# The last output part of a decoder layer's first feed-forward: loads asked for together, the third weight set summed and split ahead of two updates, and copies of the turned x on two engines

## The chip, the cores and the metric

The kernel runs on one core of one Trainium2 chip. The metric is device time in microseconds (us), as the median of several executions. TensorE (PE in the profile, PEld for its weight loads) multiplies into PSUM; VectorE (DVE) and ScalarE (ACT) do the elementwise work; GpSimd (POOL) and SyncE (SP) start most of the DMAs. Every engine takes its own instructions in the order in which they were written into its queue.

## The reference

One decoder layer over 512 tokens of width 1024, in float32: a gated feed-forward, a mixer (a state-space head group and a differential attention), a cross-attention into a memory of 256 tokens, a second gated feed-forward and a last norm.

```python
x = x + 0.5 * swiglu(rms_norm(x, norm_ffn1_w[l]), ffn1_w_in[l], ffn1_w_out[l])
x = x + hybrid_mixer(rms_norm(x, norm_mix_w[l]), ...)
x = x + memory_cross_attention(rms_norm(x, norm_cross_w[l]), rms_norm(mem, norm_mem_w[l]), ...)
x = x + 0.5 * swiglu(rms_norm(x, norm_ffn2_w[l]), ffn2_w_in[l], ffn2_w_out[l])
...
def swiglu(h, w_in, w_out):
    gate, up = jnp.split(h @ w_in, 2, axis=-1)
    return (jax.nn.silu(gate) * up) @ w_out
```

The change is in the product with `ffn1_w_out` and in what follows it directly.

## The kernel before

Every float32 operand is split into a high part (`wh`, `s31h`, ..., a copy on ScalarE) and a low part (`wl`, `s31l`, ..., source minus high, on VectorE), and each product is three passes on TensorE: high by high, low by high, high by low. The products of both feed-forwards are block products of 2 by 2 blocks with seven products in place of eight (the Strassen-Winograd form), so sums of blocks are needed on both sides: `S1` to `S4`.

The first feed-forward goes in three thirds of its 2816 hidden columns. A third first makes quads (`quad`, L260, tiles `qa`, `qe`, `qb`), which give the gated hidden blocks `th`. From the last `th` of a third the steps in `block_tiles` and `sums_in_steps` (L205) make `g11`, `s31`, `s24` and `g` with their high and low parts. Then `out_blocks` (L1287) multiplies them with the output weights into six PSUM tiles, `oa`, `oe` and `ob` for two halves each. In the last third there are four blocks k = 0 to 3, in two parts (0, 1) and (2, 3); only k = 3 comes from the last `th`. The order of the seven products is:

- `oa` with block 11 and `oe` with `S1`, part after part: 11 first part, `S1` first part, 11 second part, `S1` second part;
- a copy of `oa` into `ob` on ScalarE (L1392), two updates of `x` from `oe` on VectorE (`update`, L1334), then `ob` with `S2` ("the third weight set");
- a copy of `ob` to `u` on ScalarE (L1399) and a subtraction from `oe` on VectorE, then `oa` with block 12, `ob` with `S3`, `oe` with `S4`, `ob` with block 22, each with updates of `x` behind it.

One set of a part is 128 x 1024, loaded to a tile `wr` (512 KB) and split to `wh` and `wl`; there are six `wr` and three of each of the others. In the first feed-forward the sums of weights are made in the kernel: `S1`'s set is a load of B12 by SyncE and an adding DMA of B11 by GpSimd on top (`added`, L1342); the third set is `S1`'s plus B22, by one VectorE instruction per part (`t2`, L1353, L1355); `S3`'s is a load and an adding DMA; the set for block 22 adds B21 to the third set, in the last third by DMA (`t4`, L1366). Each matmul of these products is 128 x 512 (L1319).

Between them stand other streams: `prepare` puts four small matmuls `prel` and two ScalarE copies `hot` (L640) with two DMAs (L643) into the last third; `memory_in` (L1069) puts eight splits of the memory, `hm`, there. Behind the third, `turn` (L1251) turns x by 32 TensorE transposes into eight PSUM tiles `pxf` and copies them back (L1258); the norm of x follows (`nboth`, `nv`, `ncol`, `ndiag`, then two matmuls `nrow`), and the keys of the memory (`pck`, L146). SyncE's and GpSimd's queues stand in the order of the source; on the other engines the framework sets the order from its own model of times, and a wait is put in wherever data or a buffer asks for it. The last third of the first feed-forward is the only one with `by_dma`. The second feed-forward uses the same `out_blocks` with weight sums that lie in DRAM.

Of the kernel before, what the change touches and what calls it, by code (L numbers as in the profile page):

```python
# [18 lines left out]
T = 512  # L19
# [81 lines left out]
def body(tc, a, dbg=None):  # L101
# [38 lines left out]
    last, start, last_sum, recent, newest, newest_mm, first_block = [], [], [], [], [], [], []  # L140
# [64 lines left out]
    def sums_in_steps(b11, b21, b22, b12, pair=None):  # L205
# [9 lines left out]
        s31 = split("s31", s31)  # L215
        yield
# [852 lines left out]
    def memory_in(dst):  # L1069
        yield 9.0  # L1070
# [180 lines left out]
    def turn(n, banks=None, summed=False):  # L1251
# [5 lines left out]
        for tb in range(4):  # L1257
            S.activation(x[4 * n + tb], pt[tb], AF.Copy)  # L1258
            if summed:
                squared(4 * n + tb, x[4 * n + tb])  # L1260
            yield
# [25 lines left out]
    def out_blocks(blocks, sums, g, col4, ncol4, each=None, finale=None, clean=True, n=None, by_dma=False):  # L1287
# [14 lines left out]
        def weights(of, part, raw=None):  # L1302
# [5 lines left out]
            recent[:] = [i.ins for i in split_into(hi, lo, raw)]  # L1308
# [13 lines left out]
        def product(ps, of, which, first=False, ready=None, after=((), ())):  # L1322
            for part in parts:
                if ready and part == parts[0]:
                    w = ready
# [27 lines left out]
        def t2(part):  # L1353
            more = fetch(blocks[B22], part)
            V.tensor_tensor(t_raw[part], t_raw[part], more, ALU.add)  # L1355
            return t_raw[part]
# [11 lines left out]
        later = {}  # L1368
        here = sums is None
        if here:  # L1370
            sums = [t1, added(blocks[B12], blocks[B22], "gate"), t2, lambda part: t_raw[part]]
        ready = [None, None]
        if early:
            ready = [weights(of, parts[0]) for of in (blocks[B11], sums[0])]
            yield
        bank = [acc, aux]
# [5 lines left out]
        both = [product(a_ps, blocks[B11], "11", True, ready[0]), product(e_ps, sums[0], S1, True, ready[1], ((), tuple(first_block)))]  # L1382
# [18 lines left out]
        yield from product(a_ps, b21 if here and not by_dma else blocks[B21], "12")  # L1401
# [5 lines left out]
        for n, _ in enumerate(product(b_ps, sums[1], S3, after=(copies, ()))):  # L1407
            if n == 0:
                first_split = list(recent)
            elif n == 12 and by_dma:  # L1410
                with behind(first_split):
                    for part in t_raw:
                        t4(part)
            yield
# [182 lines left out]
```

## Time and profile before

| what | us |
|---|---|
| median of 3 runs (lowest, highest) | 1299.35 (1299.22, 1300.01) |
| the profiled execution | 1299.78 |
| its span | 1298.0 |
| TensorE busy in it | 1284.4 |
| VectorE, ScalarE, GpSimd busy | 970.5, 710.2, 119.1 |

A profile's times count from the start of the span. A row of a timeline has the start, the busy time, the engine, the line, the operation, the tile written and the tiles read, the count of instructions merged in the row, and in brackets the idle time of the engine ahead of it with what ended it. Rows overlap a little, since an instruction's end is its result's, while the engine takes the next one sooner. A row of the waits has the total, the times and the longest. A row of the windows has the stretch, its length, the busy time of an engine with its instructions, the clock that was granted to TensorE (1.00 is full), the share of the DMA engines and GB/s.

### The profile page before, as it was taken

Reading aid. Unit: us, or ns where it says so; the run is one execution under the profiler, and the core shown is the slowest. Engines: PE = TensorE matmul, PEld = TensorE weight load, DVE = VectorE, ACT = ScalarE, POOL = GpSimd, SP = SyncE. Lnnn points to the kernel's source line nnn. Section 1 sums busy time; section 2 is a strip of 40 time slices with the busy share of each in tenths; the row PEclk is TensorE's granted clock in tenths of the full one; section 3 lists DMA queues with packets and bytes.
Section 4 is the critical chain, followed back from the end, with each engine's and each line's share of the span. In section 5 each row is a group of like instructions: output and inputs, shape, how many; then the busy total and the mean of one; then the engine's idle time right before and its main releaser. Section 6 shows DMA issues by size and latency. Waiting matters only on the chain.

```text
span 1298.0 us, 20081 instructions
## 1 busy us (share of the span) xinstructions
PE 1284.4 (99%) x7709; PEld 1125.5 (87%) x7709; DVE 970.5 (75%) x1543; ACT 710.2 (55%) x1207; POOL 119.1 (9%) x149
## 2 busy tenths in 40 slices
PE   9999999999999999999999999999999999999997
PEld 7889998998888778877888888889899899989995
DVE  6988897797776676567867696645678878877886
ACT  7544564565654564346644574434466546555554
POOL 1001010001101011100102011020001000000000
PEclk9999999999999999999999999999999999999999
DMA  9468777777975436653475567693249876666662
GB/s 336 101 172 209 183 195 207 227 192 203 295 234 155 131 65 159 227 165 98 106 207 180 158 163 223 198 228 113 66 130 249 214 223 183 185 191 191 173 206 94
DMA packets 69264, 234.75 MB, mean 181 GB/s; under 512 B 8161, under 2 KB 9665, under 8 KB 68817
## 3 DMA queue, kind: packets, MB, share of 16 engines
q1 hardware_dynamic: 53200, 180.91, 41.8%
q0 software_dynamic: 13168, 45.67, 19.8%
q10 hardware_dynamic: 2800, 6.91, 1.6%
q8 instruction: 60, 0.98, 0.3%
q14 instruction: 36, 0.29, 0.1%
HBM read 231.30 MB, written 48.29 MB: 215 GB/s over the span
## 4 chain that ended last, share of the span: by engine, by line
PE 81%; issue 12%; DMA 2%; DVE 2%; POOL 1%; ACT 1%; POOLq 0%; SPq 0%; ACTq 0%; DVEq 0%
PE qb L242 11%; PE pm L146 10%; PE qe L242 8%; PE qa L242 8%; PE pxbc L146 5%; PE ob L1319 5%; PE oa L1319 4%; PE pcq L146 3%; PE oe L1319 3%; PE pz L146 3%; PE pk L146 2%; PE pq L146 2%; PE pa L146 2%; PE pcv L146 2%; PE pv L146 2%
## 5 line engine op out<-in xcount | busy, mean ns | idle before, releaser
L155 ACT ACTIVATE wh<-wr 128x1024 fp32r<-128x1024 f32 (+1 forms) x323 | 328.2, 1018 | 304.6 <-PE qe L242 37.2
L156 DVE TENSOR_TENSOR wl<-wr,wh 128x1024 fp32r<-128x1024 f32 (+1 forms) x323 | 378.4, 1175 | 99.7 <-ACT wh L155 73.0
L788 ACT ACTIVATE ec<-ec,mn 128x512 f32<-128x512 f32 (+3 forms) x64 | 35.4, 554 | 22.0 <-DVE mn L787 22.0
L787 DVE CUSTOM_DVE_ANT_0 ec<-ps,bias 128x512 f32<-128x512 f32 (+3 forms) x64 | 28.1, 487 | 16.1 <-PE ps L146 15.9
L900 DVE SCALAR_TENSOR_TENSOR conv<-pxbc,par,conv 128x511 f32<-128x511 f32 (+2 forms) x48 | 35.7, 744 | 3.5 <-ACT conv L896 2.9
L251 POOL DMA_DIRECT2D wr<-in_f2q x11 | 9.7, 879 | 307.7 <-DMA wr<-in_f2q 116.8
L366 POOL TENSOR_TENSOR ncol<-nv,mhalf 128x4 f32<-128x4 f32 (+1 forms) x9 | 11.0, 1222 | 291.1 <-DVE nv L364 291.1
L146 PE MATMUL pxbc<-hnl,wh 128*128 128x512 f32 x128 | 35.6, 404 | 0.0
L146 PE MATMUL pxbc<-hnh,wh 128*128 128x512 f32 x128 | 35.3, 400 | 0.0
L146 PE MATMUL pxbc<-hnh,wl 128*128 128x512 f32 x128 | 32.3, 393 | 0.0
L453 DVE TENSOR_TENSOR gate<-qb,row 128x512 f32<-128x512 f32 x19 | 13.1, 692 | 22.1 <-PE qb L242 22.1
L146 PEld LDWEIGHTS pxbc<-hnh,wl 128*128 128x128 f32 x128 | 23.8, 188 | 5.3 <-issue 0.2
L251 POOL DMA_DIRECT2D wr<-in_f1q x16 | 14.0, 873 | 152.2 <-DMA wr<-in_f1q 58.9
L146 PEld LDWEIGHTS pxbc<-hnl,wh 128*128 128x128 f32 x128 | 23.2, 188 | 4.7 <-issue 0.4
L146 PEld LDWEIGHTS pxbc<-hnh,wh 128*128 128x128 f32 x128 | 23.0, 189 | 4.6 <-issue 0.5
L454 ACT ACTIVATE gate<-gate 128x1024 f32<-128x1024 f32 x19 | 20.1, 1057 | 10.9 <-DVE gate L453 10.9
L146 PE MATMUL pv<-wh,hnh 128*128 128x512 f32 x64 | 25.3, 395 | 0.0
L146 PE MATMUL pv<-wh,hnl 128*128 128x512 f32 x64 | 25.2, 393 | 0.0
L855 POOL TENSOR_TENSOR rr<-ev,mhalf 128x4 f32<-128x4 f32 x8 | 8.3, 1034 | 163.1 <-DVE ev L853 163.1
L155 ACT ACTIVATE s31h<-s 128x512 fp32r<-128x512 f32 x30 | 18.7, 624 | 7.4 <-DVE s L212 4.4
L155 ACT ACTIVATE s24h<-s 128x512 fp32r<-128x512 f32 x30 | 18.8, 625 | 7.0 <-DVE s L214 7.0
L301 ACT ACTIVATE u<-qb 128x512 f32<-128x512 f32 x19 | 11.4, 598 | 19.8 <-PE qb L242 19.8
(461 smaller groups left out, 3527.9 us busy)
## 6 DMA issues: line engine op xcount, KB each, us to landing
wr<-in_f2q SPq DMA_DIRECT2D x44, 512.0 KB, 4.4
wr<-in_f1q SPq DMA_DIRECT2D x40, 512.0 KB, 4.3
wr<-in_f1b SPq DMA_DIRECT2D x25, 512.0 KB, 5.3
isum<-in_f2q SPq DMA_DIRECT2D x22, 512.0 KB, 5.4
wr<-isum SPq DMA_DIRECT2D x22, 512.0 KB, 4.2
wsum<-in_f2b SPq DMA_DIRECT2D x20, 512.0 KB, 6.3
wr<-wsum SPq DMA_DIRECT2D x20, 512.0 KB, 4.4
wr<-in_f1q POOLq DMA_DIRECT2D x16, 512.0 KB, 6.5
```

The source lines that it names most:

```text
L146: newest_mm[:] = [nc.tensor.matmul(out, w, x, start=start, stop=stop).ins]
L155: S.activation(hi, src, AF.Copy),
L156: V.tensor_tensor(lo, src, hi.bitcast(F32), ALU.subtract),
L242: newest_mm[:] = [nc.tensor.matmul(out, w_[:, wc], xs[kp][which][x_], start=first and j == 0 and f == 0 and kp == 0, stop=j == 2 and kp == ...
L251: last_sum[:] = [G.dma_start(raw, m, accum_op=ALU.add).ins]
L301: copy = S.activation(u2, b_ps, AF.Copy)
L453: V.tensor_tensor(gate[:, 2 * i : 2 * i + 2], halves(gs[i]), row, ALU.mult)
L454: S.activation(gate, gate, AF.Silu)
L787: V.tensor_tensor_reduce(out=ec[:, :n], in0=ps[c][:, parts[i]], in1=bias[:, T - n :], scale=0.125, scalar=3e38, op0=ALU.add, op1=ALU.min, ...
L788: S.activation(ec[:, :n], ec[:, :n], AF.Exp, bias=mn, scale=-1.0, accum_out=sm[c][:, i : i + 1])
L900: V.scalar_tensor_tensor(y[:, d:], ps[:, : T - d], par[:, cw + j : cw + j + 1], y[:, d:], ALU.mult, ALU.add)
L1319: newest_mm[:] = [nc.tensor.matmul(ps, a_[:, ts], b_[:, ws], start=first and k == 0 and j == 0, stop=k == n - 1 and j == 2, skip_group_che ...
```

## The change

Four edits, the first two in `out_blocks`:

1. `ask_early`, for the last third alone: the second parts of block 11 and `S1` are asked for, then B22 for both parts in four loads of 256 KB to tiles of their own (`more`), then both parts of `S3`'s set with their adding DMAs. Before, each load stood in the queue where its product was written. The additions of B22 (`t2`) become four instructions of 128 x 512 in place of two of 128 x 1024. The adding DMAs of `t4` are asked for in the product with block 12, no longer in the one with `S3`.
2. The third weight set is made (`weights`) ahead of the copies of `oa` and the two updates of x: both parts in the last third, the first part everywhere else. The low half of its first part is told to stand behind the low half of `s31` (`sums_low`); in the last third the two updates stand behind the split.
3. `turn` with banks: four of its eight copies go to VectorE.
4. `memory_in` starts 13 units of the model's time after its cue in place of 9.

```diff
+        sums_low[:] = last[1:]
...
     def memory_in(dst):
-        yield 9.0
+        yield 13.0
...
         for tb in range(4):
-            S.activation(x[4 * n + tb], pt[tb], AF.Copy)
+            if banks and tb % 2:
+                V.tensor_copy(x[4 * n + tb], pt[tb])
+            else:
+                S.activation(x[4 * n + tb], pt[tb], AF.Copy)
...
-        def weights(of, part, raw=None):
+        def weights(of, part, raw=None, low_behind=()):
...
-            recent[:] = [i.ins for i in split_into(hi, lo, raw)]
+            high = S.activation(hi, raw, AF.Copy)
+            with behind(low_behind):
+                low = V.tensor_tensor(lo, raw, hi.bitcast(F32), ALU.subtract)
+            recent[:] = [high.ins, low.ins]
...
         def t2(part):
-            more = fetch(blocks[B22], part)
-            V.tensor_tensor(t_raw[part], t_raw[part], more, ALU.add)
+            more = pieces.pop(part) if part in pieces else (fetch(blocks[B22], part),)
+            n = t_raw[part].shape[1] // len(more)
+            for i, m in enumerate(more):
+                V.tensor_tensor(t_raw[part][:, i * n : (i + 1) * n], t_raw[part][:, i * n : (i + 1) * n], m, ALU.add)
             return t_raw[part]
...
+        def ask_early():
+            for of, make in ((B11, lambda part: fetch(blocks[B11], part)), (S1, t1)):
+                asked[of, parts[1]] = make(parts[1])
+            for part in parts:
+                pieces[part] = [s2("more") for _ in range(*part)]
+                for k, m in zip(range(*part), pieces[part]):
+                    nc.sync.dma_start(m, blocks[B22][:, k * T : (k + 1) * T])
+            for part in parts:
+                asked[S3, part] = seventh(part)
...
+        if by_dma:
+            ask_early()
...
+        third = {part: weights(sums[2], part, low_behind=() if n else sums_low) for n, part in enumerate(parts if by_dma else parts[:1])}
+        third_split = list(recent) if by_dma else []
         for t in range(2):
             S.activation(b_ps[t], a_ps[t], AF.Copy)
-        for t in range(2):
-            update(t + 2, 1, e_ps[t], 1, False)
-        yield from product(b_ps, sums[2], S2)
+        with behind(third_split):
+            for t in range(2):
+                update(t + 2, 1, e_ps[t], 1, False)
+        yield from product(b_ps, sums[2], S2, ready=third)
...
-        yield from product(a_ps, b21 if here and not by_dma else blocks[B21], "12")
+        for n, _ in enumerate(product(a_ps, b21 if here and not by_dma else blocks[B21], "12")):
+            if n == 12 and by_dma:
+                for part in t_raw:
+                    t4(part)
+            yield
```

What this makes of the queues, at the places that the prediction speaks of. First VectorE, in the last third, from the low half of `S1`'s second set (the first `wl`) to the updates of x. Before, with `wr_3373` and `wr_3459` the sets of the first and second part, to which L1355 adds B22:

```order
L156 TENSOR_TENSOR wl_3463<-wr_3459,wh_3462 128x1024
L213 TENSOR_TENSOR s_598_3392<-s_597_3391,th_3381 128x256
L1355 TENSOR_TENSOR wr_3373<-wr_3373,wr_3492 128x1024
L214 TENSOR_TENSOR s_598_3392<-s_598_3392,th_3381 128x256
L156 TENSOR_TENSOR s31l_3397<-s_597_3391,s31h_3396 128x512
L1355 TENSOR_TENSOR wr_3459<-wr_3459,wr_3516 128x1024
L156 TENSOR_TENSOR s24l_3401<-s_598_3392,s24h_3400 128x512
L156 TENSOR_TENSOR wl_3496<-wr_3373,wh_3495 128x1024
L156 TENSOR_TENSOR gl_3405<-th_3381,gh_3404 128x512
L1336 SCALAR_TENSOR_TENSOR x_123<-oe_3410,col_68_292,x_123 128x512
```

And VectorE there now, with `wr_3373` and `wr_3410` as the two sets and `more` as B22:

```order
L1314 TENSOR_TENSOR wl_3477<-wr_3410,wh_3476 128x1024
L213 TENSOR_TENSOR s_598_3392<-s_597_3391,th_3381 128x256
L214 TENSOR_TENSOR s_598_3392<-s_598_3392,th_3381 128x256
L156 TENSOR_TENSOR s31l_3397<-s_597_3391,s31h_3396 128x512
L156 TENSOR_TENSOR s24l_3401<-s_598_3392,s24h_3400 128x512
L156 TENSOR_TENSOR gl_3405<-th_3381,gh_3404 128x512
L1364 TENSOR_TENSOR wr_3373<-wr_3373,more_3413 128x512
L1364 TENSOR_TENSOR wr_3373<-wr_3373,more_3414 128x512
L1364 TENSOR_TENSOR wr_3410<-wr_3410,more_3417 128x512
L1364 TENSOR_TENSOR wr_3410<-wr_3410,more_3418 128x512
L1314 TENSOR_TENSOR wl_3502<-wr_3373,wh_3501 128x1024
L1314 TENSOR_TENSOR wl_3508<-wr_3410,wh_3507 128x1024
```

All additions now stand behind `s31l`, `s24l` and `gl`, where one stood ahead of `s31l` and the other ahead of `s24l`; both low halves of the third set follow them, ahead of the updates.

ScalarE at the same place, before, from the high half of `S1`'s second set to the second part of the third set (`wh_3495` and `wh_3519` are the third set's high halves):

```order
L155 ACTIVATE wh_3462<-wr_3459 128x1024
L155 ACTIVATE s31h_3396<-s_597_3391 128x512
L155 ACTIVATE wh_3495<-wr_3373 128x1024
L155 ACTIVATE s24h_3400<-s_598_3392 128x512
L1392 ACTIVATE ob_3412<-oa_3408 128x512
L1392 ACTIVATE ob_3413<-oa_3409 128x512
L155 ACTIVATE gh_3404<-th_3381 128x512
L640 ACTIVATE hot_2459<-prel_3473 8x256
L640 ACTIVATE hot_2460<-prel_3473 8x256
L643 DMA rel_d<-hot_2459 8x256
L159 ACTIVATE hm_3478<-mem_539_3032,par 128x256
L159 ACTIVATE hm_3504<-mem_539_3032,par 128x256
```

And ScalarE there now (`wh_3501` and `wh_3507` are the third set's high halves):

```order
L1312 ACTIVATE wh_3476<-wr_3410 128x1024
L155 ACTIVATE s31h_3396<-s_597_3391 128x512
L155 ACTIVATE s24h_3400<-s_598_3392 128x512
L155 ACTIVATE gh_3404<-th_3381 128x512
L1420 ACTIVATE ob_3431<-oa_3427 128x512
L1420 ACTIVATE ob_3432<-oa_3428 128x512
L641 ACTIVATE hot_2459<-prel_3487 8x256
L641 ACTIVATE hot_2460<-prel_3487 8x256
L644 DMA rel_d<-hot_2459 8x256
L644 DMA rel_d<-hot_2460 8x256
L1312 ACTIVATE wh_3501<-wr_3373 128x1024
L1312 ACTIVATE wh_3507<-wr_3410 128x1024
```

The high half of the third set's first part has moved from the third place of this piece behind the two `hot` copies, which read `prel`, and behind both DMAs.

VectorE in the first third of the second feed-forward, before (`wl_10673` is the third set's first part, `wl_10691` its second):

```order
L156 TENSOR_TENSOR wl_10673<-wr_10670,wh_10672 128x1024
L156 TENSOR_TENSOR s31l_10583<-s_2167_10577,s31h_10582 128x512
L156 TENSOR_TENSOR wl_10691<-wr_10688,wh_10690 128x512
L156 TENSOR_TENSOR s24l_10587<-s_2168_10578,s24h_10586 128x512
L1336 SCALAR_TENSOR_TENSOR x_123<-oe_10600,col_2175_10594,x_123 128x512
```

And now (`wl_10675` is the third set's first part):

```order
L156 TENSOR_TENSOR s31l_10589<-s_2169_10583,s31h_10588 128x512
L1314 TENSOR_TENSOR wl_10675<-wr_10672,wh_10674 128x1024
L156 TENSOR_TENSOR s24l_10593<-s_2170_10584,s24h_10592 128x512
L1343 SCALAR_TENSOR_TENSOR x_123<-oe_10606,col_2177_10600,x_123 128x512
L156 TENSOR_TENSOR gl_10597<-th_10573,gh_10596 128x512
```

Here `s31l` and the third set's low half have changed places; the second part's has gone behind both updates.

Elsewhere: TensorE's queue is the same but for the two matmuls `nrow` of the memory's norm, which stood directly behind the 32 transposes and now stand behind the first 18 `pck`, and those of x's norm, which stand two `pck` earlier, counted in `pck`. In SyncE's queue the four `more` loads stand behind the first four loads of `out_blocks`, whose order is as before; behind them `S3`'s two loads, then the two of B21. The eight `hm` splits stand later on both engines.

More of the change, by code (lines that the diff above doesn't have):

```diff
@@ L1323, in product @@
             for part in parts:
-                if ready and part == parts[0]:
-                    w = ready
+                if ready and part in ready:
+                    w = ready[part]
                 else:
@@ L1381, in out_blocks @@
             nc.tensor.matmul(b_ps[1], ones_r, ones_r[:, None, :].to_broadcast([P, 4, P]), start=True, stop=True)
-        both = [product(a_ps, blocks[B11], "11", True, ready[0]), product(e_ps, sums[0], S1, True, ready[1], ((), tuple(first_block)))]
+        both = [product(a_ps, early_or(B11, lambda part: fetch(blocks[B11], part)) if by_dma else blocks[B11], "11", True, ready[0]), product(e_ps, sums[0], S1, True, ready[1], ((), tuple(first_block)))]
         for _ in parts:
@@ L1406, in out_blocks @@
             update(t, 0, a_ps[t])
[L1407 to L1414, printed above, removed]
+        yield from product(b_ps, sums[1], S3, after=(copies, ()))
         for t in range(2):
```

11 lines of the change are left out of this document (7 added, 4 removed).

## The prediction

> **What bounds the kernel now.** I read the busy times first, then TensorE's waits, then the timelines around each wait. The span, and TensorE's row in the page's busy times (time, share, instructions):
>
> ```profile
> span 1298.0 us, 20081 instructions
> ```
>
> ```profile
> PE 1284.4 (99%) x7709; PEld 1125.5 (87%) x7709; DVE 970.5 (75%) x1543; ACT 710.2 (55%) x1207; POOL 119.1 (9%) x149
> ```
>
> TensorE is busy for all but 13.6 us of the span, so only what makes it stand still, or run slower, can be won. The waits that the change can touch are one row of TensorE's list (total, times, longest):
>
> ```profile
> PE oe L1319 <- DVE s31l L156: 1.6, 2, 1.3
> ```
>
> and, behind the third, the wait in the turn of x:
>
> ```profile
> PE pck L146 <- ACT x L1258: 0.5, 1, 0.5
> ```
>
> The longest is in the last third of the first feed-forward. TensorE's timeline there:
>
> ```profile
> 309.13 0.61 PE L1319 MATMUL oe<-wh,s31l 128*128 128x512 f32 x2
> 311.00 0.50 PE L1319 MATMUL oe<-wh,s31l 128*128 128x512 f32 x1 [1.26 <-DVE s31l L156]
> 311.43 1.02 PE L146 MATMUL prel<-hot,rel_sb 32*8 32x256 f32 x4
> 312.39 0.50 PE L1319 MATMUL oe<-wh,s31l 128*128 128x512 f32 x1
> 312.73 1.42 PE L1319 MATMUL oe<-wl,s31h 128*128 128x512 f32 x4
> 313.94 1.91 PE L1319 MATMUL ob<-wh,s24h 128*128 128x512 f32 x4
> ...
> 317.08 1.07 PE L1319 MATMUL ob<-wl,s24h 128*128 128x512 f32 x4
> 317.99 1.07 PE L1319 MATMUL ob<-wh,s24h 128*128 128x512 f32 x4
> ...
> 320.71 1.07 PE L1319 MATMUL oa<-wh,gh 128*128 128x512 f32 x4
> ```
>
> Two things are seen: 1.26 us of standing still, and, three us later, four matmuls that take 1.91 us where four such take 1.07 at 317.08. Two stretches of equal length, with TensorE's busy time and the granted clock, tell why:
>
> ```profile
> 309.92:313.33 3.41, 2.33 (x9) 1.00 0.61 162
> 313.33:316.74 3.41, 3.41 (x10) 0.50 0.68 220
> ```
>
> After a stretch with 2.33 us of work in 3.41 us, the clock was half for 3.41 us, which costs 1.7 us more. So the place costs about 1.4 us by the late `s31l` and 1.7 us by the clock. The 24 matmuls of `ob` took 6.77 us (313.94 to 320.71); at full clock four of them are 0.91 us apart (317.08 to 317.99), which is 5.45 us for 24.
>
> **Part 1, the last third.** Why `s31l` was late, in VectorE's timeline, from the low half of `S1`'s second set on:
>
> ```profile
> 307.31 1.23 DVE L156 TENSOR_TENSOR wl<-wr,wh 128x1024 fp32r<-128x1024 f32 x1 [1.98 <-ACT wh L155]
> 308.45 0.42 DVE L213 TENSOR_TENSOR s<-s,th 128x256 f32<-128x256 f32 x1
> 308.79 1.22 DVE L1355 TENSOR_TENSOR wr<-wr,wr 128x1024 f32<-128x1024 f32 x1
> 309.93 0.42 DVE L214 TENSOR_TENSOR s<-s,th 128x256 f32<-128x256 f32 x1
> 310.26 0.69 DVE L156 TENSOR_TENSOR s31l<-s,s31h 128x512 fp32r<-128x512 f32 x1
> 310.86 1.22 DVE L1355 TENSOR_TENSOR wr<-wr,wr 128x1024 f32<-128x1024 f32 x1
> ```
>
> and ScalarE's, from the landing of that set on:
>
> ```profile
> 306.22 1.06 ACT L155 ACTIVATE wh<-wr 128x1024 fp32r<-128x1024 f32 x1 [1.97 <-DMA wr<-in_f1b]
> 307.19 0.62 ACT L155 ACTIVATE s31h<-s 128x512 fp32r<-128x512 f32 x1
> ...
> 313.12 0.62 ACT L640 ACTIVATE hot<-prel 8x256 f32<-8x256 f32 x2
> 313.50 0.27 ACTq L643 DMA_DIRECT2D rel_d<-hot  x1
> ```
>
> The chain begins with a landing at about 306.1. Its load is the fourth in SyncE's queue before and after, so loading at once does not move it, unless traffic does; I leave it there. From 308.45 on one L1355 addition (1.14 us, 308.79 to 309.93) goes out of the chain. The two L213 and L214 then follow each other, the second reading the first's result, so 308.45 and 0.42 and the 0.33 from L214 to `s31l` put the latter at 309.2. TensorE ran on 0.74 us after its start (310.26 to 311.00), so now at 309.95. It ran dry at 309.74 (309.13 and 0.61): 0.2 us of idle is left of 1.26.
>
> Then the new wait. From TensorE's restart to the end of the last `oe` matmul were, before, 0.43 + 0.96 + 0.34 us to 312.73, and four more at full clock 0.91: 2.64 us. So TensorE is ready for `ob` at 309.95 + 2.64 = 312.6. `ob` needs the high half of the third set's first part. On VectorE that has been put behind `s24l`, `gl` and two additions. `s24l` waits for `s24h` on ScalarE (0.62 us behind L214's end at 309.3, so 309.95); then `s24l` and `gl` at 0.60 each (the spacing behind `s31l`) to 311.15, and two additions of 128 x 512, bounded by that 0.60 from below and by half of L1355's 1.14 also at 0.57: done at 312.4. On ScalarE the set now stands behind the two `hot`, which read `prel`: `prel` ends 1.4 us after the restart (311.00 to 312.39), at 311.35; two `hot` and two DMA issues of 0.27 (the first 0.38 us behind the first `hot`) end about 1.0 us later, 312.4. Both branches give 312.4; the copy takes 1.06 us; `ob` starts at 313.55, where it started at 313.94. So TensorE stands still for about 0.95 us at `ob`, in place of 1.05 us won at `oe`. Ahead of `ob` the gain is 0.4 us, of which 0.3 was clock. The low half follows at 312.5 to 314.7 and is asked for eight matmuls after the start, 315.4: covered.
>
> What else is queued behind: the updates of x move behind both splits, to some 316, and their readers come at the product with `S3`; the `hm` splits, whose reader `pck` starts at 347; closest is B21's second split, which now stands behind both `u` and one `hm`: two copies of some 0.55 us, one of half that width and its own 1.06 are about 2.5 us behind `ob`'s end, where TensorE asks after 12 matmuls, 2.7 us. I cost these at nothing; if B21's split is late, at most its own 1.06 us.
>
> Whether the clock drops again decides as much as the wait. By the same stretch, 309.92 to 313.33, TensorE would have stood still for about 0.65 us and run `prel` (32 rows and 8 columns) for 0.96 us; before it was 1.08 and the same 0.96. If the windows fall where they fell, the stretch is a little fuller than the one that cost the clock. I take it that it drops: the half clock then takes about 1.6 us from `ob` (313.55 to 316.74), which ends at 313.55 + 5.45 + 1.6 = 320.6, against 320.71. **0.1 us won.** If it doesn't drop, 319.0, **1.7 us won.**
>
> [...]
>
> **Part 2, the second feed-forward.** The second wait of the `s31l` row, in TensorE's, ScalarE's and VectorE's timelines:
>
> ```profile
> 1028.67 0.61 PE L1319 MATMUL oe<-wh,s31h 128*128 128x512 f32 x2
> 1029.63 0.73 PE L1319 MATMUL oe<-wh,s31l 128*128 128x512 f32 x2 [0.34 <-DVE s31l L156]
> ```
>
> ```profile
> 1027.62 0.61 ACT L155 ACTIVATE s31h<-s 128x512 fp32r<-128x512 f32 x1
> ```
>
> ```profile
> 1027.75 1.23 DVE L156 TENSOR_TENSOR wl<-wr,wh 128x1024 fp32r<-128x1024 f32 x1 [0.26 <-ACT wh L155]
> 1028.89 0.69 DVE L156 TENSOR_TENSOR s31l<-s,s31h 128x512 fp32r<-128x512 f32 x1
> ```
>
> A pair of matmuls on time takes half of 0.91 us, so 1029.63 should have been 1029.12: 0.5 us lost. Now `s31l` stands ahead of the low half and waits for `s31h` alone, until 1028.2; 0.74 us later is 1028.95, in time. **0.5 us won**; between 0.34 (the idle alone) and 0.6 (a slow pair behind it). The low half of the third set goes to 1028.8 to 1030.0; `ob` starts two pairs after 1029.1, at 1030.0, and asks for that half eight matmuls (1.8 us) later: covered.
>
> **Part 3, the turn.** TensorE's timeline, and VectorE's last row ahead of its copies:
>
> ```profile
> 342.49 3.68 PE L150 MATMUL pxf<-ident,x 128*128 128x128 f32 x32
> 346.26 0.50 PE L146 MATMUL nrow<-ndiag,ones_r 128*128 128x256 f32 x2
> 347.24 2.18 PE L146 MATMUL pck<-hm,wh 128*128 128x256 f32 x16 [0.47 <-ACT x L1258]
> ```
>
> ```profile
> 344.40 1.21 DVE L156 TENSOR_TENSOR wl<-wr,wh 128x1024 fp32r<-128x1024 f32 x1
> ```
>
> `pck` needs a PSUM tile whose copy was the fourth on ScalarE. Now it takes that of the first copy on VectorE, which starts at 345.5 (344.40 and 1.13 to the next). A 128 x 512 copy out of PSUM on VectorE isn't in the trace; ScalarE's L1258 and VectorE's 128 x 512 rows put it at 0.6 to 0.7. So `pck` starts at about 346.25, 1.0 us sooner, and the two `nrow` that moved behind take 0.25 back: **0.75 us won**, between 0.3 and 0.8. The two copies ahead of `nv` delay x's norm by nearly 2 us: `nv` at 347.5, GpSimd's `ncol` 1.0 us, `ndiag` done at 350.4, where TensorE asks at 350.6 (34 `pck` and two `nrow` after 346.25). The margin is 0.2 us; without it up to 0.4 us of the gain is lost, which is in the bound.
>
> **The sum.** 0.1 + 0.5 + 0.75 = 1.35 us. On the profiled execution (1299.78, 1.8 outside the span) that is 1298.4; that execution lies 0.4 above the median, so 1298.0 on the median of 1299.35.
>
> **The rivals.** *The clock holds.* `ob` ends at 319.0, the sum is 1.7 + 0.5 + 0.75 = 2.95: 1296.4. For it speaks that the idle is split in two, so that a window holds less of it, and that the windows need not lie as they lay; against it that the low stretch is nearly as long. [...]
>
> *The sum for `S1` lands later, and it is slower than before.* The chain starts with a landing. This kernel's adding DMAs from GpSimd and their medians to landing:
>
> ```profile
> wr<-in_f1b POOLq DMA_DIRECT2D x5, 512.0 KB, 9.3
> ```
>
> ```profile
> gate<-in_f1b POOLq DMA_DIRECT2D x1, 512.0 KB, 11.5
> ```
>
> With 1 MB of `more` and half of `S3`'s set asked for at once, `S1`'s sum may take 11.5 us, 2.2 more. All of the chain follows, `ob` starts at 315.75, 1.8 later than before, with the clock lost too: 1.8 − 1.25 = +0.5 or a little more, 1300.0. It decides from 1.4 us of delay on. Against it speaks SyncE's queue of before, where two loads of 512 KB were issued ahead of the DMA of that sum (306.1 less 9.3 is 296.8) and competed with it too:
>
> ```profile
> 293.44 3.21 SPq L1299 DMA_DIRECT2D wr<-in_f1b  x2
> ```
>
> [...]
>
> *The change doesn't do what it says.* The waits only change their names: the wait at `ob` is as long as that at `oe`, and `nrow` takes the place of `pck`. Then 0.5 us in the second feed-forward stays: 1298.9.
>
> **How the numbers follow.** Forecast 0.45; the clock holds 0.35; late landing 0.10; names only 0.10. A measurement of this kernel can tell about 0.2% from no change, 2.6 us: faster is below 1296.75, slower above 1301.95. Faster: three quarters of the second case and a little of the first, 0.30. Slower: half of the late landing, when it is worse than 11.5, 0.06. The rest, 0.64, is within. The range takes the forecast and the second case, with 0.4 us of bounds below, and reaches to the late landing: 1296.0 to 1300.0.
>
> **What would show it.** Right: no idle over 0.3 us at `oe`, about 0.9 us of idle at `ob` ended by ScalarE's `wh`, a half clock behind it, no wait at the `oe` near 1029, `pck` directly behind the transposes. Wrong: no wait at `ob` (then `prel` or the additions were sooner than I count), `S1`'s set landing away from 306, or a wait at `nrow`.

## The result, and the profile after

| | kernel before | changed kernel |
|---|---|---|
| median (lowest, highest) of 17 runs | 1298.96 (1296.72, 1301.29) | 1296.62 (1295.91, 1299.70) |
| ratio, 95% interval | | 0.9984 (0.9977 to 0.9990) |
| the profiled execution, its span | 1299.78, 1298.0 | 1296.45, 1293.8 |

The change wins 2.3 us, 0.16%, with an interval from 1.3 to 3.0 us. The page's first rows, of the changed kernel:

```profile
span 1293.8 us, 20087 instructions
...
PE 1281.4 (99%) x7709; PEld 1123.9 (87%) x7709; DVE 973.1 (75%) x1549; ACT 707.6 (55%) x1203; POOL 118.0 (9%) x149
```

In its list of TensorE's waits, the rows on `oe` and `pck` are gone, and there is a new one:

```profile
PE ob L1326 <- ACT wh L1312: 0.9, 1, 0.9
```

TensorE's timeline of the last third of the first feed-forward, changed kernel (start, busy time, engine, line, operation, count, idle time ahead):

```profile
308.64 0.84 PE L1326 MATMUL oe<-wh,s31l 128*128 128x512 f32 x3
309.41 1.02 PE L146 MATMUL prel<-hot,rel_sb 32*8 32x256 f32 x4
310.37 0.50 PE L1326 MATMUL oe<-wh,s31l 128*128 128x512 f32 x1
310.70 1.09 PE L1326 MATMUL oe<-wl,s31h 128*128 128x512 f32 x4
312.65 1.20 PE L1326 MATMUL ob<-wh,s24h 128*128 128x512 f32 x4 [0.86 <-ACT wh L1312]
...
318.25 1.07 PE L1326 MATMUL oa<-wh,gh 128*128 128x512 f32 x4
```

No idle time at `oe`, 0.86 us at `ob`, and no half clock behind it (the granted clock is 1.00 in each window from 308.19 to 318.43): the 24 matmuls of `ob` take 5.60 us (312.65 to 318.25), where they took 6.77. ScalarE's and VectorE's timelines show who holds `ob`:

```profile
303.66 1.04 ACT L1312 ACTIVATE wh<-wr 128x1024 fp32r<-128x1024 f32 x1
...
310.47 0.64 ACT L641 ACTIVATE hot<-prel 8x256 f32<-8x256 f32 x2 [1.55 <-PE prel L146]
310.88 0.62 ACTq L644 DMA_DIRECT2D rel_d<-hot  x2
311.54 2.01 ACT L1312 ACTIVATE wh<-wr 128x1024 fp32r<-128x1024 f32 x2 [0.43 <-DVE wr L1364]
```

```profile
306.69 0.69 DVE L156 TENSOR_TENSOR s31l<-s,s31h 128x512 fp32r<-128x512 f32 x1
...
308.68 2.49 DVE L1364 TENSOR_TENSOR wr<-wr,more 128x512 f32<-128x512 f32 x4
```

The first two of the four additions were done at 309.9 (308.68 and half of 2.49), yet `wh` began at 311.54: it stood behind `hot` and its DMAs, as those stood behind `prel`. The bracket names VectorE; by the times it was ScalarE's own queue. And `S1`'s second set was there earlier than I counted with: ScalarE's copy of it, `wh` at 303.66, waits for nothing; before, it waited until 306.22.

The turn (first the changed kernel, then the row of before that answers to its last), and the second feed-forward:

```profile
340.01 3.65 PE L150 MATMUL pxf<-ident,x 128*128 128x128 f32 x32
343.42 2.16 PE L146 MATMUL pck<-hm,wh 128*128 128x256 f32 x16
...
348.98 1.12 PE L146 MATMUL pck<-hm,wl 128*128 128x256 f32 x8
```

```profile
352.59 1.12 PE L146 MATMUL pck<-hm,wl 128*128 128x256 f32 x8
```

```profile
1025.04 0.62 PE L1326 MATMUL oe<-wh,s31h 128*128 128x512 f32 x2
1025.51 0.63 PE L1326 MATMUL oe<-wh,s31l 128*128 128x512 f32 x2
```

`pck` follows the transposes directly, `oe` near 1025 without a gap. Of the two spans' difference, 0.46 us lies ahead of everything that was changed, in the first matmuls, so it is no part of the change (before, then after):

```profile
6.49 1.09 PE L146 MATMUL pa<-hml,wah 128*128 128x512 f32 x4
```

```profile
6.03 1.07 PE L146 MATMUL pa<-hml,wah 128*128 128x512 f32 x4
```

| place | before | after | won, us |
|---|---|---|---|
| start of `ob`, counted from those first matmuls | 307.45 | 306.62 | 0.83 |
| `ob`'s 24 matmuls | 6.77 | 5.60 | 1.17 |
| from there to the transposes | 21.78 | 21.76 | 0.02 |
| first transpose to the `pck` behind x's norm | 10.10 | 8.97 | 1.13 |
| pair of `oe` in the second feed-forward | 0.96 | 0.47 | 0.49 |

That is 3.6 us in one pair of profiles, and 2.3 in the medians. The pair must not be taken for the typical case: most executions of the kernel before don't have the half clock that makes the second row (worked out with e4), and in a second profile of it (e7) the stretch of the turn is 9.53 us (341.95 to 351.48), which leaves 0.56 of the 1.13. The runs below show what else varies.

### The profile page after: what moved, and what is told of

It is laid out like the page before. It is cut to its first block, busy times and chain, and to the rows that moved or that the text cites. A ratio compares the mean times of both kernels' runs of the same rounds, so it can differ in the third digit from the quotient of the medians.

```text
span 1293.8 us, 20087 instructions
## 1 busy us (share of the span) xinstructions
PE 1281.4 (99%) x7709; PEld 1123.9 (87%) x7709; DVE 973.1 (75%) x1549; ACT 707.6 (55%) x1203; POOL 118.0 (9%) x149
## 4 chain that ended last, share of the span: by engine, by line
PE 87%; issue 9%; ACT 1%; DVE 1%; DMA 1%; POOL 1%; POOLq 0%; ACTq 0%; SPq 0%
PE qb L243 13%; PE pm L146 10%; PE qe L243 8%; PE qa L243 8%; PE ob L1326 6%; PE pxbc L146 5%; PE oa L1326 5%; PE oe L1326 4%; PE pcq L146 3%; PE pz L146 3%; PE pk L146 2%; PE pq L146 2%; PE pcv L146 2%; PE pa L146 2%; PE pv L146 2%
```

## The experiments

All medians, with the ratio to the kernel before on the same chip. In the expectations "squares of the memory" stands for edit 4, the memory's splits and norm at 13 in place of 9, and "third part" for edits 3 and 4 together.

| run | median (runs) | ratio, 95% interval |
|---|---|---|
| e1: before with edits 3 and 4 | 1299.77 (11) | 1.0005 (0.9996 to 1.0014) |
| e2: changed, `prel` late | 1297.82 (11) | 0.9992 (0.9984 to 1.0001) |
| e3: before, `prel` late | 1298.59 (11) | 0.9997 (0.9989 to 1.0006) |
| e4: changed, one copy twice | 1300.17 (11) | 1.0006 (0.9996 to 1.0016) |
| e5: changed, third set's first part ahead | 1295.07 (9) | 0.9970 (0.9961 to 0.9980) |
| e6: changed, without edit 3 | 1297.05 (11) | 0.9990 (0.9981 to 1.0000) |
| e7: before again | 1299.03 (1) | |
| e8: changed again | 1296.36 (11) | 0.9984 (0.9975 to 0.9993) |
| e9: changed, without edit 4 | 1297.56 (11) | 0.9992 (0.9983 to 1.0001) |
| e10: changed, without edits 3 and 4 | 1298.16 (11) | 0.9997 (0.9988 to 1.0006) |
| e11: changed, second feed-forward as before | 1297.12 (11) | 0.9984 (0.9976 to 0.9993) |
| e12: changed, without edit 1 | 1298.15 (11) | 0.9994 (0.9985 to 1.0003) |

My theory after the result: the wait at `ob` comes by ScalarE's queue, the clock holds because less of a window is lost, and the turn's 1.1 us come from the copies on VectorE. Rivals: VectorE's additions hold `ob`; the early landing is the work of loading at once; the place of `nrow` makes the turn.

### Landing, and the same kernels again: e7 and e8

> The kernel before, unchanged, for a second profile. Theory: the place of S1's landing differs by some 3 us from run to run (ScalarE's copy of it starts at 303.6 to 306.6 in six profiles so far), so the wait at oe and the half clock behind it need not be there: an idle anywhere from 0 to 1.3 us. Rival: with SyncE's loads as they are before, the landing lies near 306 each time, and the idle of about 1.2 us comes again.

> The changed kernel, unchanged, for a second profile and its times on this chip. Theory: the landing varies here too, but s31l no longer stands behind an addition, so oe waits 0.3 us or less wherever it falls; the wait at ob is between 0.8 and 1.7 us and grows with the landing; 1297 us or so. Rival: loading at once brought the landing forward to 303 for good, and the profile shows the wait of 0.86 us at ob again, no more.

The kernel before again: nearly the same idle time at `oe`, and the same half clock, so this pair of profiles fits e7's rival. TensorE's timeline, ScalarE's copy of the set, and the two windows:

```profile
310.46 0.50 PE L1319 MATMUL oe<-wh,s31l 128*128 128x512 f32 x1 [1.16 <-DVE s31l L156]
```

```profile
305.68 1.06 ACT L155 ACTIVATE wh<-wr 128x1024 fp32r<-128x1024 f32 x1 [1.87 <-DMA wr<-in_f1b]
```

```profile
308.48:311.89 3.41, 2.25 (x10) 0.85 (x8) 3.41 (x5) 2.30 (x4) 0.00 (x0) 1.00 0.38 88
311.89:315.30 3.41, 3.41 (x9) 2.76 (x9) 3.34 (x6) 3.32 (x8) 1.14 (x2) 0.50 0.67 249
```

In the changed kernel again, the same copy came at 305.60, 1.9 us later than in its first profile (TensorE was 0.9 us later there by a wait far ahead of the place), and yet `oe` didn't wait, and `ob` waited the same; e8's rival, an early set for good, is out:

```profile
305.60 1.06 ACT L1312 ACTIVATE wh<-wr 128x1024 fp32r<-128x1024 f32 x1 [0.89 <-DMA wr<-in_f1b]
```

```profile
313.60 1.21 PE L1326 MATMUL ob<-wh,s24h 128*128 128x512 f32 x4 [0.86 <-ACT wh L1312]
```

Over all profiles that copy starts between 303.6 and 306.6 with the loads of before (306.2, 305.7, 305.9, 303.6, 304.4) and with the new ones (303.7, 304.8, 306.6, 304.4, 305.6, 305.6, 305.8, 306.3, 306.6) alike. Up to 1.2 us of the spread is the program's own start (the first matmuls shown above lie at 5.91 to 7.14). Counted from there, the copy starts between 297.6 and 299.7; the four early ones wait for nothing, so their sets had landed sooner still, and at least 2 us are the landing's. Much of it is there before the adding DMA begins: GpSimd started it at 294.13 to 295.06 in those four profiles and at 295.26 to 297.83 in the other ten. So loading at once did not bring `S1`'s landing forward; the early one in the first profile was one draw of several. What the change does is to bear a late one: e9, e10 and e11 have sets as late as the kernel before and no wait at `oe`.

### The clock and the wait at ob: e2, e3, e4

e2 and e3 put `prel` behind the newest matmul of `ob` (after and before alike):

```
-        yield 9.0
+        yield 17.0
         prel = aux("prel", (8, T))
-        for i in range(2):
-            mm(prel[:, i * H : (i + 1) * H], rel_sb, hot[i], True, True)
+        with behind(list(newest_mm)):
+            for i in range(2):
+                mm(prel[:, i * H : (i + 1) * H], rel_sb, hot[i], True, True)
```

> The changed kernel with the matmuls prel put some 38 matmuls later, among those of ob and oa, so that ScalarE's hot copies and their DMAs stand behind the third set's high halves. Theory: the wait of 0.86 us at ob came by ScalarE's queue (wh stood behind hot, hot behind prel), the additions were done at 309.9 already; the copy now runs at about 310.0 and the wait falls to at most 0.4 us; 0.5 to 0.8 us less than the changed kernel. Rival: VectorE's additions held it; then TensorE, which reaches ob 0.96 us sooner without prel, waits 1.4 to 1.8 us there, and the time is that of the changed kernel.

> The kernel before with prel put later in the same way; s31l is as late as it was, so about 1.2 us of idle stay at oe, but the window of the clock then holds no matmul of 32 rows. Theory: such narrow matmuls count as little work, so it was idle and prel together that cost the clock; it now holds at 1.00 and the time is 1.7 us less than before. Rival: an idle of over 1 us in a window is enough; the clock goes to 0.50 for 3.41 us again, and the time is that of the kernel before.

e4 makes the copy for the third set's first high half twice:

```
-            high = S.activation(hi, raw, AF.Copy)
+            for _ in range(2 if again else 1):
+                high = S.activation(hi, raw, AF.Copy)
```

> The changed kernel with the copy that makes the high half of the third set's first part done twice, which delays ob by one copy of 0.97 us, so that TensorE stands still for 1.8 us there. Theory: prel ends ahead of the wait, and idle time of itself takes the clock when a window has more than about 1.1 us of it; 1.8 us is enough, the clock goes to 0.50 for a window, and the time is 0.97 + 1.7 = 2.7 us more than the changed kernel. Rival: idle without narrow matmuls beside it doesn't count, the clock holds, and it is 1.0 us more.

e2, the wait, VectorE's additions, and the window of the wait:

```profile
312.32 1.21 PE L1327 MATMUL ob<-wh,s24h 128*128 128x512 f32 x4 [1.66 <-ACT wh L1313]
```

```profile
309.83 2.49 DVE L1365 TENSOR_TENSOR wr<-wr,more 128x512 f32<-128x512 f32 x4
```

```profile
308.89:312.30 3.41, 1.77 (x8) 1.13 (x6) 3.41 (x7) 2.24 (x4) 0.88 (x1) 1.00 0.99 335
```

My theory lost: with `prel` out of the way `ob` waits longer, for the first two additions, done at 311.1 (309.83 and half of 2.49), and the copy behind them. ScalarE's copy of `S1`'s set had started 1.15 us later than in the changed kernel's first profile (304.81), and the additions 1.15 us later. So ScalarE's and VectorE's ways to `ob` are of nearly one length with such a landing, and shortening one of them wins next to nothing (`ob` started 0.33 us sooner than in the changed kernel, with `prel`'s 0.96 still to come). In the medians e2 is 1.2 us above the changed kernel, with intervals that overlap.

The same window tells about the clock: 1.66 us of standing still in one window, and the clock was 1.00, behind it too (the next four matmuls take 1.21 us, where they took 1.91 at half clock in the kernel before). The kernel before lost it with 2.33 and 2.25 us of work in a window, more than the 1.77 here. The difference is `prel`: in the window of before it is 1.02 us of those 2.33,

```profile
309.92:313.33 3.41, 1.02 (x4) 0.26 (x4) 0.21 (x1) 1.00 0.61 162
```

which leaves 1.31 us of full matmuls (1.25 in e7, by the same subtraction). e4 had `prel` and idle time in one window too:

```profile
310.56:313.97 3.41, 2.59 (x10) 1.12 (x9) 3.41 (x6) 2.96 (x6) 0.01 (x1) 1.00 1.05 268
```

1.57 without `prel`'s 1.02, and it held (the mean granted clock of that execution is 0.998). So the clock fell at 1.25 and 1.31 us of full matmuls in 3.41 us and held at 1.57 and 1.77. My reading of these four windows is a clock that goes by work done, with `prel`'s matmuls of 32 rows and 8 columns as hardly any. The traces hold more windows that can tell. At the end of the program the last full matmuls fill only a part of a window, with no `prel` near: e1, where the clock then fell, and e8, where it held for one window more. And e10 had `prel` and a long wait in one window, and held (its next window is at 1.00 too):

```profile
1287.64:1291.05 3.41, 1.09 (x5) 0.56 (x3) 3.00 (x7) 2.57 (x6) 1.16 (x2) 1.00 0.80 302
1291.05:1294.46 3.41, 0.00 (x0) 0.00 (x0) 0.49 (x1) 0.72 (x1) 0.27 (x1) 0.50 0.82 308
```

```profile
1285.08:1288.50 3.42, 1.60 (x8) 0.99 (x6) 3.10 (x8) 2.27 (x6) 0.80 (x2) 1.00 0.65 243
1288.50:1291.91 3.41, 0.00 (x0) 0.00 (x0) 0.87 (x2) 1.13 (x2) 0.72 (x1) 1.00 0.82 309
```

```profile
310.36:313.77 3.41, 2.50 (x10) 1.12 (x9) 3.05 (x6) 2.52 (x7) 0.18 (x1) 1.00 1.04 329
```

By the time in full matmuls the order is clean: the clock fell after 1.09, 1.25 and 1.31 us and held after 1.48 (e10 without `prel`'s 1.02), 1.57, 1.60 and 1.77. By busy time with `prel` in full it isn't: 2.25 and 2.33 fell where 1.60 and 1.77 held. So `prel` counted for little, if for anything; of these seven windows the three that fell have 1.31 us or less, the four that held 1.48 or more.

Both profiles of the kernel before have the half clock, but most of its executions have not. One window at half takes 0.0013 off the mean granted clock (half of 3.41 in 1298). The two profiles with one have a mean of 0.9967 and 0.9965, the twelve others of the study 0.9973 to 0.9984, so an execution that is listed with 0.998 has lost none. Of the 91 executions of the kernel before that ran beside the experiments, 57 are listed with 0.998. In most executions, then, the 1.17 us in the table above are no part of what the change wins.

e4's wait of 1.97 us was split by a window's edge in the profiled run (0.8 us before 313.97). The edges don't lie at one place of the program. In the kernel before the clock fell a second time at 1292.95, behind the last matmuls, 286 times 3.413 us after the edge at 316.74; in the changed kernel it fell at 1287.83, and as many windows ahead of that is an edge at 311.60. Counted from the first matmuls, that is 305.57, where the one at 313.33 of the kernel before is 306.84. e4's executions fall in two groups: six of eleven took 1300.2 to 1302.8 with a mean granted clock of 0.996 or less, five 1296.9 to 1299.0 with 0.997 or more. That the place of the edge parts them is an estimate of mine from the one execution that was profiled. Gaps of 1.66 us in e2 and 0.86 us in the changed kernel did not cost the clock; 1.26 and 1.16 us in the kernel before, with `prel` in the same window, did, and at the end of e1 it fell 2.3 us after the last matmul (1288.73 to 1291.05).

Neither of e4's forecasts holds for all its executions. e3 told nothing on this: its set landed early (ScalarE's copy at 303.56), and there was no idle time at `oe` to judge.

### The first part of the third set ahead: e5

The wait at `ob` has two ways, so e5 shortens both: the first part's additions go directly behind `g11l`, its high half behind `s31h` and ahead of `hot`. The first part never needed `S1`'s second set. For this the loads of block 11, `S1` and B22 are asked for sooner as well (SyncE's first `more` at 288.52, in the changed kernel at 292.90), so e5 doesn't part the order from the loads.

```
+            if waiting and not apart:
+                with behind(first_block):
+                    waiting.pop()()
...
+                            third[parts[0]] = weights(None, parts[0], summed[parts[0]], sums_low, sums_high)
+                            ahead[:] = recent
...
+            with behind(ahead[:1]):
+                S.activation(hot[i][:8], prel[:, i * H : (i + 1) * H], AF.Copy, scale=-8.0)
```

> The changed kernel with the additions of B22 to the third set's first part moved ahead, directly behind g11l on VectorE, its high half on ScalarE directly behind s31h and ahead of the two hot, its low half behind s31l. Theory: the third set's first part never needed S1's second set, it only stood behind it and behind prel in the two queues; with both ways shortened the wait at ob goes (0.86 us in the changed kernel, 1.66 with prel late) and oe starts as it did: 0.9 us less than the changed kernel, near 1295.7. Rival: the two additions ahead of the sums delay s31l by their 1.2 us, a wait at oe of 0.3 to 0.9 us takes the place of that at ob, and the time is that of the changed kernel.

```profile
311.47 1.09 PE L1331 MATMUL oe<-wl,s31h 128*128 128x512 f32 x4
312.40 1.07 PE L1331 MATMUL ob<-wh,s24h 128*128 128x512 f32 x4
```

```profile
307.39 1.04 ACT L1317 ACTIVATE wh<-wr 128x1024 fp32r<-128x1024 f32 x1
```

`wh` is done four microseconds before it is asked for, TensorE waits at neither place, and the median of 1295.07 is the lowest of the study, 1.3 to 1.6 us under the changed kernel's where 0.9 was expected; the range of its nine runs is 1.4 us where that of the kernel before is 4 to 5 in its larger numbers of runs. The theory holds at `ob` and `oe`; what the earlier loads add is not shown.

### The loads: e1 and e12

> The kernel before with the third part of the change alone: two of the four copies of turned x on VectorE, and the memory's squares 4 us later. Theory: pck starts directly behind the transposes, and the two nrow behind them wait for nothing, so the stretch from the first transpose to the pck behind x's norm is 1.1 us shorter, the time 1.1 us less (ratio 0.9991). Rival, the prediction's sum: 0.75 us (0.9994). Beside it, the landing of S1's second set: near 306 and an idle of 1.2 us or so at oe if only loading at once brought it forward in the changed kernel; near 303 and less idle if its place differs from run to run.

e12 takes the call of `ask_early` out and puts `t4` back into the product with `S3`:

```
-        if by_dma:
-            ask_early()
```

> The changed kernel without the loads at once: B22, S3 and the DMAs that add to them are asked for where they were, the additions again stand ahead of s31l; the third set still goes ahead of the updates, and the turn is as changed. Theory: S3's second set lands near 327 as in the kernel before, so whatever is won at oe is lost by a wait of 0.8 us or more at ob behind it, ended by that set's high half, and at oe there is again up to 1.2 us of idle; 1.5 us or more over the changed kernel, that is near the time of the kernel before. Rival: the order of the third set makes the gain; no wait over 0.3 us at that ob, and the time is that of the changed kernel.

Here e12's set landed early (304.37), so neither `oe` nor the first `ob` waited at all. Then, in its list of TensorE's waits, and in ScalarE's timeline:

```profile
PE ob L1326 <- ACT wh L1312: 0.8, 1, 0.8
PE pxf L150 <- DVE x L1343: 0.6, 2, 0.3
PE pck L146 <- DVE x L1260: 0.2, 1, 0.2
```

```profile
325.89 1.06 ACT L1312 ACTIVATE wh<-gate 128x1024 fp32r<-128x1024 f32 x1 [2.39 <-DMA gate<-in_f1b]
```

`wh<-gate` is the high half of `S3`'s second set. `ob` with `S3` waits 0.82 us for it at 327.00. Behind it in ScalarE's queue stand the copies that later products wait for, and the transposes and `pck` wait for VectorE's updates and copy of x. e1 shows the same waits (0.8, 0.6 and 0.2 us), and with them no gain: its median of 1299.77 is not below the kernel before, and both its forecasts failed. The kernel before comes close to this bound too, just behind the stall at `oe`:

```profile
327.62 1.06 ACT L155 ACTIVATE wh<-gate 128x1024 fp32r<-128x1024 f32 x1 [2.42 <-DMA gate<-in_f1b]
```

```profile
328.87 1.08 PE L1319 MATMUL ob<-wh,s31h 128*128 128x512 f32 x4
```

The copy ends at 328.68, and TensorE, late by the lost clock, takes it at 328.87: no idle time is shown, and more than 0.2 us could not be won ahead of it unless the copy came sooner too. With the loads at once the same copy starts in the changed kernel without a wait:

```profile
322.29 1.05 ACT L1312 ACTIVATE wh<-gate 128x1024 fp32r<-128x1024 f32 x1
```

where TensorE asks at 326.40. So edit 1 is worth 1.5 to 1.8 us in the medians (1298.15 against 1296.62 and 1296.36) and 1.3 by the ratios, whose intervals overlap. In this profile it comes by the landing of `S3`, whose adding DMA GpSimd started at 308.94 in the changed kernel, at 316.05 in the kernel before and at 314.02 in e12. What a late `S1` would cost e12 at `oe`, where its additions stand ahead of `s31l` again, no profile shows.

### The turn and the memory's splits: e6, e9, e10

```
-            if banks and tb % 2:
-                V.tensor_copy(x[4 * n + tb], pt[tb])
-            else:
-                S.activation(x[4 * n + tb], pt[tb], AF.Copy)
+            S.activation(x[4 * n + tb], pt[tb], AF.Copy)
```

is e6 and half of e10; `yield 9.0` for 13.0 in `memory_in` is e9 and the other half.

> The changed kernel with all four copies of turned x on ScalarE again; the order of TensorE is unchanged. Theory: the third part's 1.1 us came from the copies; a wait of about 0.8 us at pck comes back (the fourth copy ends 1.1 us later, nrow no longer stands between), and the time is 0.8 us more than the changed kernel. Rival: with nrow behind the pck, and the copies ready sooner because the squares end sooner, ScalarE alone is in time: under 0.3 us of wait and no difference.

> The changed kernel with the memory's squares at their old time (9 in place of 13), so that its two nrow stand directly behind the transposes again; copies on both engines as in the change. Theory: nrow takes the tile of one copy and pck that of the next but one; with VectorE's second copy ready at 343.7 that costs only the two nrow and no wait, at most 0.3 us. Rival: the place of nrow made the whole gain of the turn; pck waits as before and about 1 us is lost.

> The changed kernel without the third part: all copies on ScalarE and the memory's squares at their old time. Theory: with nrow ahead, pck has to wait for ScalarE's fourth copy, about 2.0 us after its first, which starts 2.0 us behind the first transpose; TensorE then loses 0.4 us at pck and 0.25 by the nrow, 0.7 us more than the changed kernel. Rival: the 1.1 us seen between the two first profiles come back in full.

e6, TensorE and ScalarE:

```profile
340.49 3.65 PE L150 MATMUL pxf<-ident,x 128*128 128x128 f32 x32
343.90 2.16 PE L146 MATMUL pck<-hm,wh 128*128 128x256 f32 x16
```

```profile
342.53 3.99 ACT L1259 ACTIVATE x<-pxf 128x512 f32<-128x512 f32 x8
```

`pck` comes 3.41 us after the first transpose, as in the changed kernel. With `nrow` behind it, `pck` starts when two of ScalarE's copies are done (at 343.6), and no longer waits for the fourth. The copies on VectorE bought nothing once `nrow` had moved: the rival holds.

e10 waits again at `pck`, which comes 4.14 us after the first transpose; of the 0.73 us lost, 0.2 come back where the two `nrow` stood in the changed kernel (the stretch to the `pck` behind x's norm is 9.49 us, against 8.97):

```profile
342.19 3.65 PE L150 MATMUL pxf<-ident,x 128*128 128x128 f32 x32
...
346.33 2.18 PE L146 MATMUL pck<-hm,wh 128*128 128x256 f32 x16 [0.25 <-ACT x L1259]
```

e9 has no such wait, as the theory said. But both lose more, 0.85 us, at a place that neither expectation named. e9, TensorE and VectorE:

```profile
314.12 1.19 PE L1326 MATMUL ob<-wh,s24h 128*128 128x512 f32 x4 [1.71 <-ACT wh L1312]
```

```profile
310.85 0.68 DVE L1364 TENSOR_TENSOR wr<-wr,more 128x512 f32<-128x512 f32 x1
311.89 0.48 DVE L160 SCALAR_TENSOR_TENSOR hm<-mem,par,hm 128x256 fp32r<-128x256 f32 x1 [0.36 <-ACT hm L159]
312.30 1.89 DVE L1364 TENSOR_TENSOR wr<-wr,more 128x512 f32<-128x512 f32 x3
```

With the memory's splits at their old time one of them stands between the first addition and the second: 0.85 us with its own wait for ScalarE (1.45 between the two starts, 0.60 without it), and `ob` waits 1.71 us in place of 0.86. e10 has the same split there, and 1.72 us of waiting. Edit 4 keeps it away. So the third part's worth, 1.5 to 1.8 us in the medians (1298.16 against 1296.62 and 1296.36), lies more at `ob` than at the turn, where it is 0.5.

### The second feed-forward: e11

> The changed kernel with the third set's low half free to stand ahead of s31l in the thirds of the second feed-forward, as before. Theory: TensorE waits 0.3 us at oe near 1025 again and the place is 0.5 us longer. Rival: the wait is a matter of how the run falls, and the place is as short as now.

```profile
1027.57 0.73 PE L1326 MATMUL oe<-wh,s31l 128*128 128x512 f32 x2 [0.34 <-DVE s31l L156]
```

The wait is back to the hundredth, and the pair before it had started at 1026.62, 0.95 us ahead where the changed kernel has 0.47. In the medians 0.5 us can't be told from nothing (the ratio is that of the changed kernel).

## Why the prediction was right, and where not

The time was forecast at 1298.0 with a range of 1296.0 to 1300.0, and is 1296.62. The direction and range were right. The likeliest case was not the one that came: it was the second, *the clock holds*, with 1296.4. That this number is so near is in part luck: its sum counts 1.6 us for a half clock that most executions of the kernel before don't have, and leaves out what edits 1 and 4 win at places that it did not cost.

- **The idle time at `oe`.** 0.2 us of 1.26 was to be left; it is 0 in two profiles of the changed kernel, 0.16 in e6's. The reason was right: one addition went out of the chain. In the changed kernel's first profile the early set would have done it too; e9, e10 and e11 have it at 305.8 to 306.6 and no wait either, and there only the reason is left.
- **The landing "at about 306", not moved by loading at once.** Not moved by it, but not fixed either: it varies by 2 us or more, which a single profile of before doesn't show. By the prediction's own sign, a landing away from 306, this part was wrong in the changed kernel's first profile.
- **The new wait at `ob`, 0.95 us, ended by ScalarE's `wh`.** It is 0.86, 0.86 and 0.87 us (changed kernel twice, e11), 0.91 in e6. The prediction's rows give 312.4 + 1.06 = 313.46 for `ob`'s start, where it wrote 313.55; the sum without the slip is 0.86. That ScalarE's and VectorE's ways end nearly together was right for a late set: in e8 the two additions are done at 311.9 (310.62 and half of 2.49) and the copy starts at 312.5. In the first profile, with the early set, VectorE was done 1.6 us ahead.
- **"I take it that it drops."** This step failed. It compared windows by busy time, `prel` counted in full, and found after hardly better than before. By the time in full matmuls its own window was better by far: 0.65 us of idle and 1.02 of `prel` leave 1.74 us, where before it was 1.31, and every window seen with 1.48 or more kept the clock. It also took one profile's half clock for the rule of the kernel before, where at least 57 of 91 executions have none. The clock held in all eight profiles with a wait at the first `ob`.
- **The second feed-forward, 0.5 us.** 0.49, and 0.5 back in e11.
- **The turn, 0.75 us, by VectorE's copies.** 1.13 in the first pair, but 0.56 against e7 and 0.52 between e10 and the changed kernel. In the first profile `nrow` too had been late (3.77 us after the first transpose, 3.41 in e7), which the prediction did not see; its cause was off as well: `nrow`'s place did it (e6), the copies only serve where `nrow` stands ahead (e9 against e10).
- **What I costed at nothing.** That the `hm` splits stand later, taken for harmless, is worth 0.85 us at `ob` (e9). That `S3`'s loads stand earlier was not costed at all; edit 1, which does it, is worth 1.3 to 1.8 us (e12).

The last point is the one that matters. I took the stall at `oe` and its clock for time that comes back when they go. In the profile of the kernel before, `S3`'s set was ready at 328.68, 0.2 us ahead of its use, and in e7 0.8 us ahead (the copy ends at 327.59, TensorE takes it at 328.35). A TensorE that comes sooner than that meets the next wait unless this set comes sooner too, and e12 and e1 show that wait, 0.82 us in each. The bound is not fixed: in e3, where `S1`'s set was early, the same copy started at 324.10, and TensorE took its tile at 325.21 with no wait in its list. So how much of the stall's time would have been lost again is argued, not shown. Edit 1 moved that second bound out of the way. The parts don't add: before with the third part is 1.0005, the change without it 0.9997, the change without the loads 0.9994, all with intervals that hold 1; together they are 0.9984.

Still open: what the clock counts exactly, what edit 2 is worth alone in the last third, which no run leaves out, and why `S1`'s adding DMA starts and lands so differently.

## What to carry to other kernels

Before a stall is counted as a gain, look for the next producer that comes in just in time behind it; a wait of zero in the profile of a late kernel is a bound that is not seen yet. Where two engines' queues reach one instruction at the same time, shorten both or neither, as e5 did with work that was ready long before. And compare several profiles of the kernel before: a landing that varies by 2 us makes any sum from one of them a draw, and a half clock that both profiles show can still be missing from most executions.

## What the runs showed of the hardware

- The clock went to 0.50 for a window of 3.41 us after 2.33 us (kernel before) and 2.25 us (e7) of busy time in the window ahead, 1.0 of it in matmuls of 32 rows and 8 columns (1.31 and 1.25 us without them), and after 1.09 us of full matmuls alone (end of e1); it stayed at 1.00 after 1.48 (e10), 1.57 (e4), 1.60 (end of e8) and 1.77 us (e2) of full ones. By busy time alone 2.25 and 2.33 us fell where 1.60 and 1.77 held.
- While the adding DMA of `S1`'s second set was under way in the kernel before (296.85 to 306.12), the DMA engines were busy for 0.83 of the time, at 220 GB/s. From 296 to 310 it was 0.61, at 170 GB/s, and 0.58, at 151, in e7. Whether their rate held the set back, no run tests.
